# The low part of every fourth piece of weights: a subtraction on VectorE, or a DMA that adds

## The chip, the cores and the metric

The kernel runs on one core of one Trainium2 chip. The time is device microseconds of one execution. The kernel before was run three times: 2742.07, 2743.56 and 2744.54 us, a median of 2743.56.

## What is computed

The reference is a model of two times two layers on 256 tokens of width 1024, all in float32. Each of the first two layers is a gated feed-forward of hidden width 2816, a mixer of three kinds of attention (a difference of two softmaxes, a stick-breaking one, and one by blocks), and another feed-forward; the last two have a scan with decays and a dilated-window attention as their mixer. Norms stand ahead of each phase:

```
x = x + 0.5 * rms_norm(swiglu(rms_norm(x, g1), wg, wu, wd), g2)
x = x + rms_norm(mixer(rms_norm(x, g3), w_in, ...) , g4)
x = x + 0.5 * rms_norm(swiglu(rms_norm(x, g5), wg, wu, wd), g6)
```

What matters here is that every product with weights is a float32 product, and that each weight is used once, for all 256 tokens.

## The kernel before, in words

The host lays the weights out in the order of their use, as 448 units of 512 rows by 512 columns, 1 MB each. A unit makes two *pieces* of 256 rows, so there are 896 pieces; a piece is two chunks of 128 rows.

The kernel feeds TensorE with a shorter format than float32 (float32r). Each operand is split into a high part, rounded to float32r, and a low part, what the rounding left; three products (high by high, high by low, low by high) replace one. For activations this is done once for a phase. For weights it is done piece by piece, just ahead of their use:

- `fetch` (line 395) issues the DMA of a unit on SyncE's queue (SP) into one of three `raw` buffers.
- `prepare` (line 406) takes the next piece, gets a buffer each of `whi` and `wlo` (eight of each) and calls `split`. Its instructions get a lower priority than what the program puts down after them (`LATER = 200`). While a chain of norms between two phases is under way, a piece is split in two halves of 512 elements a partition.
- `split` (line 431) is two instructions: a cast on ScalarE (ACT), raw to `whi`, and a subtraction on VectorE (DVE), raw minus `whi` to `wlo`.
- `get` hands out chunks, `pump` prepares another piece when buffers are free, and is called after each step of products.

All products go through `mm` (tokens as the stationary side, 512 weight columns moving), or `across` (weights stationary, both parts of the tokens moving). In `ahead`, `branch`, `out_proj` and the end of a down projection all chunks of up to 16 are held while the first token tile passes over them, and each is released in the pass of the second.

The order of the program is made by a planner (`_Order`, line 135). The products are its main line. Other work (norms, transposes, attention heads) is in tasks, which are taken up between steps of the main line once what they read should be there, by rough lengths of the instructions that `_Eng` (line 253) reckons for each engine. A norm's last step, `rstd` (line 463), is a power on GpSimd (POOL), which does nothing else in this kernel. Behind the planner a scheduler puts each engine's instructions into queues, which run in order.

Of the kernel before, what the change touches and what calls it, by code (L numbers as in the profile page):

```python
# [28 lines left out]
def _constants():  # L29
    """tables that depend on shapes alone"""  # L30
    i = np.arange(128)
# [28 lines left out]
def _weights(m, which=None):  # L60
    """the weights in the order of their use, by 512 rows of 512 columns: [n, 128, 4, 512]"""
    out = []
# [72 lines left out]
class _Order:  # L135
    """The order of the program. A main line of products, and tasks that are taken up between its
    steps once what they read should be there, by rough lengths of the instructions (ns)."""
    MARGIN = 300.0
# [31 lines left out]
    def table(self, fn):  # L170
        """the time to change the scalar engine's function table, if this function asks for it"""
        sets = {AF.Exp: ("exp", "ln"), AF.Ln: ("ln",), AF.Silu: ("silu",), AF.Sigmoid: ("sigmoid",)}
        need = sets.get(fn[0]) if fn else None
        if need is None or self.act in need:
            return 0.0
        self.act = need[0]
        return 1300.0
# [64 lines left out]
    def flow(self, items, limit):  # L242
        """the items' tasks, so many at a time"""
        ts = []
        for g in items:
            while sum(not t.done for t in ts) >= limit:
                yield 300
            ts.append(self.spawn(g))
            yield 300
        yield from self.until(ts)  # L250


class _Eng:
    """An engine whose instructions are put down in the order's clock."""

# [3 lines left out]
    def __getattr__(self, fn):  # L259
        f, o, k = getattr(self._e, fn), self._o, self._k  # L260

        def call(*a, **kw):
# [17 lines left out]
            elif k == "A":  # L280
                cost = 190.0 + 0.84 * n + 95.0 * max(len(aps) - 2, 0) + o.table(a[2:3])
            elif k == "G":
                cost = 500.0 + 2.2 * n
            elif fn == "tensor_tensor_scan":
                cost = 80.0 + 2.1 * n
            elif fn == "reciprocal":
                cost = 100.0 + 6.3 * n
            elif fn in ("tensor_copy", "tensor_scalar", "memset") and not psum:
                cost = 70.0 + 0.55 * n
            else:  # L290
                cost = 80.0 + 1.05 * n + (80.0 if psum else 0.0)
# [5 lines left out]
class _Net:  # L297
# [4 lines left out]
    def __init__(self, tc, ctx, ap, out):  # L302
# [9 lines left out]
        self.fetched, self.units = 0, ap["weights"].shape[0]  # L312
        self.raws, self.parts, self.held = [], [], 0
        self.chains = []
        self.setup()

# [1 line left out]
    def tile(self, name, shape, dt=F32):  # L318
# [38 lines left out]

# [1 line left out]
    def setup(self):  # L359
# [33 lines left out]

# [1 line left out]
    def fetch(self):  # L395
        """the next 512 rows' transfer; the first ones in halves, to have them sooner"""
        if self.fetched < self.units and len(self.raws) <= 2 * (self.BUFS["raw"] - 1):
# [8 lines left out]
    def prepare(self):  # L406
        """the next 256 rows' parts"""
        self.fetch()
        raw = self.raws.pop(0)
        hi, lo = self.tile("whi", [2, 512], R32), self.tile("wlo", [2, 512], R32)  # L410
        n = 2 if all(t.done for t in self.chains) else 1
        with self.tc.high_priority(offset=-self.LATER):
            for i in range(0, 2, n):
                self.split(hi[:, i:i + n], lo[:, i:i + n], raw[:, i:i + n])
        self.fetch()
# [7 lines left out]
    def get(self, n=1):  # L423
        """the (hi, lo) parts of the next n times 128 rows"""
        while len(self.parts) < n:
# [8 lines left out]

# [1 line left out]
    def mm(self, out, a, b, start, stop, last):  # L436
        """in three passes over parts; last: the weights' last use"""
        (ah, al), (bh, bl) = a, b
# [9 lines left out]
    def mf(self, out, a, b, start, stop):  # L448
        """float32 as it is: products too narrow to gain from parts"""
        self.o.tensor.matmul(out, a, b, start=start, stop=stop, skip_group_check=True)  # L450
# [7 lines left out]
    def turned(self, src, n, hi, lo):  # L458
        """src [128, n*128] transposed by blocks, in two parts"""
        self.split(hi, lo, self.transposes(src, n))  # L460

# [1 line left out]
    def rstd(self, ss, n, mult, add):  # L463
        """(ss*mult + add) ** -0.5"""
        nc = self.o
# [6 lines left out]
    def rstd2(self, ss, mult, add):  # L472
        """the same of the sum of ss's two columns"""
        ms = self.t1(1, "ms2")
# [3 lines left out]
    def pre_norm(self, t, gain):  # L478
        """x's norm, in two halves, into hT as they come"""
        nc = self.o  # L480
# [19 lines left out]
    class Finish:  # L500
        """what follows a phase: its result into x, and the next phase's norm"""

# [47 lines left out]

# [1 line left out]
    def silu(self, g):  # L552
# [10 lines left out]
    def both(self, done=None):  # L563
        """the next 512 columns for both token tiles, chunk by chunk"""
        A = [self.acc() for _ in range(2)]
# [8 lines left out]
    def across(self, done):  # L574
        """the next 512 columns as channels by tokens, 128 at a time: the weights' high part
        meets both parts of the tokens at once, their products side by side in a bank"""
        A = [self.acc() for _ in range(4)]
# [20 lines left out]
    def ahead(self, prev, done):  # L598
        """the next twice 512 columns, one token tile after the other"""
        w = {}  # L600
# [85 lines left out]

# [1 line left out]
    def gates(self):  # L688
# [7 lines left out]
    def branch(self, acts, nk, sg, first, last):  # L696
        """merged (+)= sigmoid(gate) * (acts @ w); the last one's result goes on to mT"""
        nc = self.o
# [36 lines left out]

# [1 line left out]
    def values(self):  # L737
# [4 lines left out]
    def scores(self, q, k, rows, p, mask):  # L742
        """masked scores of a map per range of rows, each in a bank of its own: blocks (queries,
        keys) = (0, 0), (1, 0), (1, 1)"""
        Z = [self.tp([3, 128]) for _ in rows]
# [12 lines left out]
    def exps(self, Z, nm, sm):  # L758
        """nm: minus the maxima per query tile, sm: the sums; -> the exponentials [128, 3, 128]"""
        nc = self.o  # L760
# [13 lines left out]
    def weigh(self, O, W, V, c):  # L774
        """O [128, 2 query tiles, n] = the weights' products with columns c of the values"""
        self.mf(O[:, 0], W[:, 0], V[:, 0, c], True, True)
# [3 lines left out]
    def weigh_fm(self, Ws, V, p, T):  # L780
        """the same for a pair of heads, channels by tokens, in two parts"""
        O = self.tp([256])
# [13 lines left out]
    def head_norm(self, O, mult, add, gain, into):  # L796
        """O [128, h, 128] in PSUM: rms norm of each head times gain"""
        nc = self.o
# [8 lines left out]

# [1 line left out]
    def rope16(self, v, t):  # L809
        """v: [128, 8, 64], the first 16 of each 64 turned"""  # L810
        nc = self.o
# [9 lines left out]
    class Heads64:  # L821
        """-> [128 (pair of heads), 4 pairs, 256 tokens], turned by their positions"""

# [52 lines left out]
    def stick(self, q, k, V, T):  # L876
        """weights sigmoid(z) times the product of sigmoid(-z) over the later keys"""
        nc = self.o
# [96 lines left out]

# [1 line left out]
    def lower_bounds(self):  # L977
        """lb of layer 1 per channel, [128, 8 heads], and 1 - lb"""
        nc = self.o
# [16 lines left out]
    def hgrn_heads(self, l, b):  # L996
        """heads 4b .. 4b+3, channels by tokens: q, f, 1 - f"""
        nc = self.o
# [18 lines left out]
    def hgrn(self, qfk, vals, b, gain, o):  # L1017
        """The scan as masked products: for a key s and a query t, the decay between them is cut
        at the largest block border between the two, so that both factors are products of f
        inside a block. o: [128 tokens, 512] per token tile, before the gate."""  # L1020
        nc = self.o
# [59 lines left out]
    class Heads128:  # L1081
        """-> [128, 4 heads, 256 tokens], normed, turned by their positions"""

# [25 lines left out]
    def dilated(self, g, q, k, V, res):  # L1109
        """group g's softmax, as unscaled sums, their weights' sums and minus their maxima"""  # L1110
        nc = self.o
# [17 lines left out]
    def joined(self, res, T):  # L1129
        """the three groups' softmaxes weighted by their sums"""  # L1130
        nc = self.o
# [80 lines left out]

# [1 line left out]
    def phases(self):  # L1214
        """[(gain of the norm ahead, body(prev, finish), gain behind, half)]"""
        ap = self.ap
# [61 lines left out]
```

## Time and profile before

| | us |
|---|---|
| median of three runs | 2743.56 |
| profiled execution: span from the first to the last instruction | 2741.8 |
| the same execution's busy time: TensorE products | 2711.4 |
| VectorE | 1839.4 |
| ScalarE | 1483.1 |
| GpSimd | 93.8 |

The profiled execution's span stands for its own time: the launch around it is not in the trace, and the median of the runs is 1.8 us above the span. Engines are PE (TensorE's products), PEld (its weight loads, beside PE), DVE, ACT, POOL and SP. A tile's name stands for all of its buffers. All instructions of the other engines have one line in the profile, L293, where `_Eng` puts them down, and all products L275; so groups are told apart by tiles (`wlo`, `whi`, `raw`, `acc`, `tp`). "<-" with a time behind it is idle time of the engine, and what ended it. 487 MB came over the DMA queues, nearly all on SP's.

### The profile page before, as it was taken

To read this page: it belongs to the slowest core of one execution; us is meant where nothing else is said; L and a number is where in the kernel's file an instruction comes from. 1 tells how busy PE (TensorE), PEld (TensorE's weight loads), DVE (VectorE), ACT (ScalarE), POOL (GpSimd) and SP (SyncE) were. 2 spreads that over 40 slices of the span, in tenths; PEclk is the share of its full clock that TensorE was granted. 3 is DMA by queue.
4 is the path that set the end of the run, shared out by engine and by line. 5 is a ranking of instruction groups with operands and counts; after the bars stand their busy time and mean duration, and the time that the engine had idled before them with its cause. 6 is when DMAs were issued, how large, how long until landed. Compare 5 with 4: busy or idle time off the path is not lost.

```text
span 2741.8 us, 36153 instructions
## 1 busy us (share of the span) xinstructions
PE 2711.4 (99%) x14152; PEld 2280.3 (83%) x14152; DVE 1839.4 (67%) x2720; ACT 1483.1 (54%) x2325; POOL 93.8 (3%) x88
## 2 busy tenths in 40 slices
PE   8999999999999999999999999999999999999999
PEld 7888778888887778888887888888888888888887
DVE  6657766666657766765666778666656578786663
ACT  6545655655646554554554555555546464564562
POOL 0000000000000100000001010000000011000000
PEclk9999999999999999999999999999999999999999
DMA  7544444555555444554554344445555453335453
GB/s 273 203 173 179 153 160 183 202 197 197 188 184 186 142 160 159 220 195 170 214 191 165 142 154 149 174 169 207 187 192 196 162 199 123 127 143 200 184 192 115
DMA packets 72602, 487.31 MB, mean 178 GB/s; under 512 B 9456, under 2 KB 11376, under 8 KB 15344
## 3 DMA queue, kind: packets, MB, share of 16 engines
q1 hardware_dynamic: 72432, 485.01, 48.3%
q8 instruction: 111, 1.82, 0.3%
q14 instruction: 59, 0.48, 0.0%
HBM read 483.93 MB, written 1.05 MB: 177 GB/s over the span
## 4 chain that ended last, share of the span: by engine, by line
PE 92%; DVE 5%; issue 1%; POOL 1%; ACT 1%; DMA 1%; SPq 0%; POOLq 0%; DVEq 0%; ACTq 0%
PE acc L275 84%; PE tp L275 7%; DVE wlo L293 1%; DVE s L293 1%; POOL rstd L293 1%; DVE big L293 1%; DVE x L293 0%; DVE ssh L293 0%; DMA raw<-in_weights_dram 0%; DVE ms L293 0%; DVE half L293 0%; DMA gain<-in_attn_q_norm_dram 0%; ACT s L293 0%; ACT p L293 0%; ACT whi L293 0%
## 5 line engine op out<-in xcount | busy, mean ns | idle before, releaser
L293 DVE TENSOR_TENSOR wlo<-raw,whi 128x1024 fp32r<-128x1024 f32 (+1 forms) x941 | 1085.0, 1170 | 486.0 <-ACT whi L293 482.2
L293 ACT CAST whi<-raw 128x1024 fp32r<-128x1024 f32 (+1 forms) x941 | 933.0, 1009 | 569.9 <-PE acc L275 473.3
L275 PE MATMUL acc<-hT,whi 128*128 128x512 f32 x2688 | 941.2, 394 | 0.0
L275 PE MATMUL acc<-whi,hT 128*128 128x512 f32 x2432 | 800.4, 398 | 0.8 <-ACT hT L293 0.6
L275 PE MATMUL acc<-hT,wlo 128*128 128x256 f32 x2688 | 753.1, 280 | 0.0
L275 PE MATMUL acc<-whi,big 128*128 128x512 f32 x2048 | 646.1, 392 | 0.0
L275 PEld LDWEIGHTS acc<-hT,whi 128*128 128x128 f32 x2688 | 503.3, 187 | 111.8
L275 PEld LDWEIGHTS acc<-whi,hT 128*128 128x128 f32 x2432 | 456.9, 188 | 96.3 <-issue 1.7
L275 PEld LDWEIGHTS acc<-hT,wlo 128*128 128x128 f32 x2688 | 508.2, 189 | 0.6
L275 PE MATMUL acc<-wlo,hT 128*128 128x512 f32 x1216 | 476.1, 392 | 0.0
L275 PEld LDWEIGHTS acc<-whi,big 128*128 128x128 f32 x2048 | 384.5, 188 | 79.2 <-issue 0.3
L275 PE MATMUL acc<-wlo,big 128*128 128x512 f32 x1024 | 399.0, 390 | 0.0
L275 PEld LDWEIGHTS acc<-wlo,hT 128*128 128x128 f32 x1216 | 229.4, 189 | 42.0
L275 PEld LDWEIGHTS acc<-wlo,big 128*128 128x128 f32 x1024 | 192.4, 188 | 38.5
L293 POOL TENSOR_TENSOR rstd<-ms,nhalf 128x1 f32<-128x1 f32 (+1 forms) x84 | 93.6, 1114 | 2466.1 <-DVE ms L293 2460.8
L293 DVE TENSOR_TENSOR s<-acc,s 128x256 f32<-128x256 f32 (+1 forms) x304 | 132.0, 435 | 66.9 <-ACT s L293 60.6
L293 ACT COPY s<-acc 128x256 f32<-128x256 f32 x288 | 106.5, 370 | 122.3 <-PE acc L275 120.6
L275 PE MATMUL tp<-big 128*128 128x64 f32 (+7 forms) x896 | 114.1, 290 | 2.5 <-ACT p L293 1.3
L275 PEld LDWEIGHTS tp<-big 128*128 128x128 f32 (+4 forms) x896 | 95.1, 184 | 18.4 <-issue 5.9
L293 ACT ACTIVATE s<-acc 128x512 f32<-128x512 f32 x88 | 52.5, 597 | 105.6 <-PE acc L275 105.3
L275 PE MATMUL tp<-c_ident,s 128*128 128x128 f32 x448 | 68.9, 278 | 23.3 <-DVE s L293 18.2
L275 PEld LDWEIGHTS tp<-c_ident,s 128*128 128x128 f32 x448 | 53.0, 142 | 42.7 <-DVE s L293 21.5
(118 smaller groups left out, 1384.9 us busy)
## 6 DMA issues: line engine op xcount, KB each, us to landing
raw<-in_weights_dram SPq DMA_DIRECT2D x446, 1024.0 KB, 4.8
gain<-in_g_ffn_pre_dram SPq DMA_DIRECT2D x4, 512.0 KB, 5.2
raw<-in_weights_dram SPq DMA_DIRECT2D x4, 512.0 KB, 9.0
gain<-in_g_ffn_post_dram SPq DMA_DIRECT2D x4, 512.0 KB, 5.6
gain<-in_ffn_norm_dram SPq DMA_DIRECT2D x4, 512.0 KB, 4.2
gain<-in_g_mix_pre_dram SPq DMA_DIRECT2D x2, 512.0 KB, 6.0
gain<-in_g_mix_post_dram SPq DMA_DIRECT2D x2, 512.0 KB, 4.3
gain<-in_mix_norm_dram SPq DMA_DIRECT2D x2, 512.0 KB, 4.4
```

What stands on the lines that cost most here:

```text
L275: return f(*a, **kw)
L293: return f(*a, **kw)
```

## The change

From the ninth piece on, each piece whose number leaves 3 by division by four (counted from 0: 11, 15, ... 895; 222 pieces) gets its low part in another way. ACT casts raw to `whi` as before, in one instruction of 1024 elements a partition; ACT then writes minus `whi` into `wlo`; then a DMA issued by GpSimd reads the same 256 rows of weights from HBM and adds them to what lies in `wlo`. The unit's transfer into `raw` is unchanged. The planner reckons 1500 ns of GpSimd for the issue, and has the low part ready 5000 ns behind it. (The diff also drops comments and docstrings.)

```diff
+            elif k == "G" and fn == "dma_start":
+                o.op("G", 1500.0, out, ins)
+                o.ready[_name(out)] = o.last[_name(out)] = o.free["G"] + 5000.0
+                return f(*a, **kw)
             elif k == "G":
                 cost = 500.0 + 2.2 * n
...
-        self.raws, self.parts, self.held = [], [], 0
+        self.raws, self.parts, self.held, self.prepared = [], [], 0, 0
...
         n = 2 if all(t.done for t in self.chains) else 1
+        u, self.prepared = self.prepared, self.prepared + 1
         with self.tc.high_priority(offset=-self.LATER):
-            for i in range(0, 2, n):
-                self.split(hi[:, i:i + n], lo[:, i:i + n], raw[:, i:i + n])
+            if u >= 8 and u % 4 == 3:
+                self.split_by_dma(hi, lo, raw, self.ap["weights"][u // 2][:, u % 2 * 2:u % 2 * 2 + 2])
+            else:
+                for i in range(0, 2, n):
+                    self.split(hi[:, i:i + n], lo[:, i:i + n], raw[:, i:i + n])
...
+    def split_by_dma(self, hi, lo, raw, src):
+
+        self.o.scalar.copy(hi, raw)
+        self.o.scalar.activation(lo, hi.bitcast(F32), AF.Copy, scale=-1.0)
+        self.o.gpsimd.dma_start(lo, src, accum_op=OP.add)
```

## Rows read from the trace of the kernel before

**Rows 1.** The page's engines: busy us, share of the span, instructions.
```profile
PE 2711.4 (99%) x14152; PEld 2280.3 (83%) x14152; DVE 1839.4 (67%) x2720; ACT 1483.1 (54%) x2325; POOL 93.8 (3%) x88
```
**Rows 2.** Busy time by stretch; PEclk is the granted clock, DMA the engines' busy share.
```profile
core 0: us, PE busy (x) PEld busy (x) DVE busy (x) ACT busy (x) POOL busy (x), PEclk, DMA share, GB/s
20.00:2730.00 2710.00, 2694.35 (x14084) 2267.11 (x14083) 1828.79 (x2701) 1472.14 (x2308) 92.49 (x82) 1.00 0.49 177
```
**Rows 3.** PE's waits between 20 and 2730 us: us, times, longest.
```profile
PE tp L275 <- DVE s L293: 7.8, 9, 1.2
PE tp L275 <- DVE ms L293: 3.8, 4, 1.7
PE tp L275 <- ACT p L293: 1.3, 2, 0.7
PE tp L275 <- DVE big L293: 1.1, 4, 0.4
PE tp L275 <- DVE half L293: 1.0, 1, 1.0
```
**Rows 4.** ACT's casts of weights in the waits of all engines.
```profile
ACT whi L293 <- PE acc L275: 473.3, 450, 5.3
...
ACT whi L293 <- DMA raw<-in_weights_dram: 25.9, 19, 5.3
```
**Rows 5.** Timeline (start, us taken): casts and first reads, pieces 167 and 603.
```profile
503.83 2.00 ACT L293 CAST whi<-raw 128x1024 fp32r<-128x1024 f32 x2 [2.45 <-PE acc L275]
...
521.96 0.28 PE L275 MATMUL acc<-hT,wlo 128*128 128x256 f32 x1
...
1842.30 1.06 ACT L293 CAST whi<-raw 128x1024 fp32r<-128x1024 f32 x1 [0.31 <-PE acc L275]
...
1851.15 0.28 PE L275 MATMUL acc<-hT,wlo 128*128 128x256 f32 x1
```
**Rows 6.** Groups by form: count, busy us, mean ns, idle before.
```profile
L293 DVE TENSOR_TENSOR wlo<-raw,whi 128x1024 fp32r<-128x1024 f32 x851 | 1027.8, 1221 | 486.0 <-ACT whi L293 482.2
...
L293 ACT CAST whi<-raw 128x1024 fp32r<-128x1024 f32 x851 | 882.7, 1051 | 564.5 <-PE acc L275 469.3 <-issue 65.8 <-DMA raw<-in_weights_dram 25.9
...
L293 ACT CAST whi<-raw 128x512 fp32r<-128x512 f32 x90 | 50.5, 615 | 5.4 <-PE acc L275 4.0 <-ACT s L293 1.4
```
**Rows 7.** Timeline of a joint between two phases, by engine.
```profile
643.87 0.68 DVE L293 TENSOR_TENSOR wlo<-raw,whi 128x512 fp32r<-128x512 f32 x1
644.47 0.14 DVE L293 TENSOR_SCALAR ms<-ms 128x1 f32<-128x1 f32 x1
...
643.15 3.73 ACT L293 CAST whi<-raw 128x512 fp32r<-128x512 f32 x7
...
646.46 0.66 PE L275 MATMUL tp<-c_ident,s 128*128 128x128 f32 x4 [1.08 <-DVE s L293]
```
**Rows 8.** POOL's powers, the tile `rstd`: ns min/median/max, first and last start.
```profile
L293 POOL TENSOR_TENSOR rstd<-ms,nhalf x84: 548/1006/2449, 8.9 to 2558.7; 128x1 f32<-128x1 f32 x52, 128x4 f32<-128x4 f32 x32
```
**Rows 9.** Timeline of one of these powers, and of VectorE beside it.
```profile
652.25 1.40 POOL L293 TENSOR_TENSOR rstd<-ms,nhalf 128x1 f32<-128x1 f32 x1 [6.63 <-DVE ms L293]
...
652.02 1.22 DVE L293 TENSOR_TENSOR wlo<-raw,whi 128x1024 fp32r<-128x1024 f32 x1
```
**Rows 10.** DMA queues (packets, MB, share); issues (count, KB, us to landing).
```profile
q1 hardware_dynamic: 72432, 485.01, 48.3%
...
raw<-in_weights_dram SPq DMA_DIRECT2D x446, 1024.0 KB, 4.8
...
out_dram<-x SPq DMA_DIRECT2D x4, 256.0 KB, 2.0
```
**Rows 11.** The tile `raw`: SP's issues in ns, then the transfers' time to landing.
```profile
L293 SPq DMA_DIRECT2D raw<-in_weights_dram x450: 327/328/1037, 2.6 to 2702.5; - x150
...
DMA to landing us min/median/max: 4.6/4.8/11.7
```
**Rows 12.** Busy time in a stretch behind a pass that held sixteen chunks.
```profile
466.00:471.00 5.00, 5.00 (x24) 4.14 (x23) 4.56 (x6) 1.50 (x5) 1.40 (x1) 1.00 0.85 316
```

## The prediction

> **What bounds the kernel now.** I read the shares of the engines first: VectorE (DVE) is busy for 67% of the span and ScalarE (ACT) for 54% [rows 1]. Then the same by stretch: between 20 and 2730 us TensorE (PE) is busy for 2694.35 of 2710.00 us [rows 2]. So 15.7 us are idle there; the other 15 us of idle time are the start and the end, which the change, beginning at the ninth piece, leaves alone. The list of PE's waits in that stretch says what the 15 us are: five entries, 15.0 us, every one in front of a product that writes a `tp` bank (transposes and attention), none for the parts of weights [rows 3]. VectorE's subtraction, however long, is not waited for. TensorE's granted clock in it was 1.00, the 2.4 GHz level [rows 2].
>
> **How far ahead the weights are.** A piece (256 rows) is cast by ACT into one of eight `whi` buffers as soon as PE has read the piece that had the buffer before: 450 casts waited for PE, 473.3 us in all [rows 4]. The time from a cast's end to PE's first read of the same piece's `wlo` is the room that a slower way to make the low part has. I paired casts and products by counting them along their engines. Of the 896 pieces the change touches 222 (numbers 11, 15, ... 895). Piece 167, a usual one, is the second cast of its row, ends at 505.83 and is first read at 521.96: 16.1 us, which is the median. Piece 603, the tightest, ends at 1843.36 and is read at 1851.15: 7.8 us [rows 5]. Of the 222, 4 have under 8 us, 15 under 9, 36 under 10, 44 under 12, 58 under 14, 92 under 16, 170 under 18. The tight ones stand behind passes that hold sixteen 128-row chunks for the first token tile and release them, fast, during the second.
>
> **The change part by part.** All sums are against the profiled execution, 2741.8 us of span; the median of the runs is 1.8 us more, and I add these 1.8 at the end.
>
> *Removed:* 222 subtractions of 1.22 us [rows 6], some 271 us of VectorE. In the bulk nobody waits for them: worth nothing. At the joints between phases, where a norm runs through ACT, VectorE and GpSimd (POOL) while PE runs out of work, a little comes back. There PE stood still 1.08 us for the normed `s`, and just before it a `ms` of the same norm had stood behind a 0.68 us subtraction [rows 7]. The power on POOL stood too: issued 0.23 us into a 1.22 us subtraction it took 1.40 us, where the shortest of its kind takes 0.55 [rows 8, 9]. There are 11 joints. A quarter of (1.22 + 0.85) us at each is 5.7 us, the most that can come back; 0 is the least; I take 2, because most of what a norm waits for is itself.
>
> The Trainium skill, "SBUF — State Buffer", section "Who interferes with whom", says that a DVE instruction with two SBUF inputs contends with a GpSimd instruction that reads SBUF but not with one that only writes it; the POOL row agrees for the reading half (1.40 against 0.55 us). By that rule the writing of a DMA's descriptors on POOL isn't held by a subtraction; if it is held like the power it costs up to 0.99 us more a DMA, which is priced below as part of the lag.
>
> *Added on ACT:* 222 copies with a factor of -1 of 128x1024. Nearest row: the cast of that shape, 1.05 us [rows 6], together 233 us, ACT 54 to 63%. In the bulk ACT waits for PE anyway [rows 4]. At a joint it can cost: seven half casts stand in a row there, 3.73 us, beside the norm's own work [rows 7]. Normally the piece is cast in two halves of 0.62 us during a chain of norms [rows 6]; a piece of the new kind takes two whole instructions of 1.05: 2.1 instead of 1.2 us, 0.9 more on ACT before a norm's next step. Eleven joints with 0 to 0.9 us each, 0 to 10 us; I take 4, a little under half, since not each piece stands ahead of a step that PE waits for.
>
> *Added on POOL and its queue:* 222 issues. The trace has none. Below: SP's issue of a weight transfer, 0.33 us; above: POOL's longest power, 2.45 us. I take 1.0, POOL's median [rows 8, 11]. Behind such an issue only POOL's 84 powers can be queued; who waits for them is the norm's next product on VectorE, and PE behind that (a rival below).
>
> *Added to the DMA engines:* 222 times 0.52 MB from HBM, added to what lies in `wlo`. Before: 485.01 MB took 48.3% of the engines [rows 10], so 116 MB more is 12%, or 23% if the destination has to be read as well. 71% in all: the engines don't become the bound on that count. Time from issue to landing: below, the 256 KB store, 2.0 us; above, the longest weight transfer, 11.7; nearest, a 1 MB transfer, 4.8, since 0.5 MB of source and 0.5 MB of destination are 1 MB of reading [rows 10, 11]. But the tight places are those where the raw buffers are being refilled: the share of the DMA engines was 0.85 in such a stretch [rows 12]. So I take 6.0.
>
> The Trainium skill, "DMA: Bandwidth & Descriptors", section "Anatomy of one DMA — SWDGE (gpsimd) path", gives 2.0 us plus the bytes over 436 GB/s, by its figures an estimate of 4.4 us for 1 MB read; no run here shows it for an adding transfer, and by it no piece would be late.
>
> *The added wait:* PE's product with `wlo` now waits for copy + issue + landing behind the cast: 1.05 + 1.0 + 6.0 = 8.05 us; ends 1.05 + 0.33 + 2.0 = 3.4 and 1.05 + 2.45 + 11.7 = 15.2. I walked through the 222 leads in order, each stall of PE pushing later casts and reads alike. PE's stalls then sum to: lag up to 7.8 us, nothing; 8 us, 0.7 us (4 pieces); 9 us, 10.6 (15); 10 us, 28 (35); 11 us, 57 (42); 12 us, 90 (43); 15.2 us, 216 (53). What is queued behind a stalled product is all of PE. I take the 8.05 and 1 us.
>
> *Moved:* the raw half is free after the cast, not after the subtraction, so SP may issue some fetches 1.2 us earlier; PE doesn't wait for raw (ACT does, 25.9 us, hidden by the leads [rows 4]): nothing. The planner that writes the order counts 1500 + 5000 ns for the new DMA: in its clock some pieces come late, and it may place a transpose of a norm a step sooner or later. I put this into the bounds of the ACT term at the joints (-4 to +10 more) with a middle of 0.
>
> Sum: 2741.8 - 2 + 4 + 1 = 2744.8, with the 1.8 us 2746.6, say **2747**: 0.1% above, within what can be told from no change (0.2%, 5.5 us).
>
> **The rivals.**
>
> 1. *The low part lands too late* (slower). One mechanism: a lag above 7.8 us stalls PE at the tight places behind the passes that hold sixteen chunks. It decides from about 8.6 us on, where it costs over 5 us. For it: landing took up to 11.7 us, and in these places the engines are filled with raw transfers. Against: the usual 1 MB landing is 4.8 us. With a lag of 10 to 11.5 us: 2747 + 27 to 73, 2774 to 2820.
>
> 2. *POOL as a queue* (slower). A power behind an issue that waits for ACT's copy comes later by up to copy plus issue, 2.1 us, at 11 joints: +23, 2770. For it: POOL runs in order, and at the joint ACT's casts and the norm's powers fall into the same 5 us [rows 7]. Against: most of the 222 issues fall between joints, with no power near.
>
> 3. *The joints get shorter* (faster). VectorE freed from the subtraction lets the powers through: POOL's rows show it held by one [rows 9]. With all 5.7 us, no ACT cost and no late piece: 2738; with the planner's 4 as well, 2734. Against: the quarter that goes is seldom the one in the way, and ACT pays more than VectorE gets.
>
> 4. *The adding is slow in the DMA engines themselves.* At five times the engine time of a byte, 58% beside the 48.3%, the engines are over full: 2742 x 1.06 = 2910 and more. Nothing in the trace bears on an adding transfer; only the factor of two has a reason in it.
>
> **How the numbers follow.** Forecast as summed 0.47, rival 1 0.30, rival 2 0.10, rival 3 0.10, rival 4 0.03. Faster by over 0.2% is rival 3: 0.10; within 0.2% the forecast: 0.47; slower by over 0.2% the rest: 0.43. The likeliest case alone reaches from 2740 to 2750 (its terms at -4 to +5 us). The range goes down to 2738, the forecast's terms with the joints' whole gain, and up to 2790, a lag of 10.5 us; beyond it lie the later part of rival 1 (0.06), rival 4 and the lower end of rival 3 (0.03).
>
> **What would show it.** VectorE's `wlo` group should fall by 222 instructions and some 271 us, ACT grow by some 233 us, POOL's queue show 222 issues with their time to landing. Step by step: if issue to landing is near 6 us and PE's list of waits still has no entry for weights, the forecast's path is right. An entry of PE for a DMA or for `wlo`, in stretches like 1843 to 1856 us, is rival 1; its size against the landing time tests the table of lags. Longer waits of PE in front of the `tp` transposes, with POOL's or ACT's new instructions ahead of the norm, are rival 2 or a larger ACT term; shorter ones are rival 3. A DMA share near 1 would be rival 4. The forecast is wrong if the time leaves 2738 to 2749 for any of these, and wrong in its reason if it stays while PE waits for `wlo`.

## The result and the profile after

The changed kernel took 2808.9 us (median of four runs, 2805.7 to 2812.1) against 2743.9 (four runs): 1.0238 times as long, 95% interval 1.0226 to 1.0249, or 65 us more. The forecast was 2747, and at most 2790. The first rival, a low part that lands too late, is what happened, within its price of 2774 to 2820 us.

What the change says it does it does: VectorE's subtractions of whole pieces fell from 851 to 642 and those of halves from 90 to 64, which is 222 pieces fewer:

```profile
L297 DVE TENSOR_TENSOR wlo<-raw,whi 128x1024 fp32r<-128x1024 f32 x642 | 778.5, 1222 | 594.1 <-ACT whi L297 593.6
L297 DVE TENSOR_TENSOR wlo<-raw,whi 128x512 fp32r<-128x512 f32 x64 | 41.3, 683 | 0.0
```

VectorE's whole busy time fell by 243 us, ACT's grew by 209, POOL's by 179 (page: busy time of the engines, then the DMA queues with packets, MB and share of the engines; q0 is POOL's; to compare with [rows 1, 10]):

```profile
PE 2733.9 (97%) x14152; PEld 2289.3 (81%) x14152; DVE 1596.4 (57%) x2485; ACT 1691.7 (60%) x2530; POOL 272.6 (10%) x310
...
q1 hardware_dynamic: 72432, 485.01, 48.6%
q0 software_dynamic: 31968, 116.41, 22.6%
```

PE is busy for 22.5 us more though it has the same 14152 products, and the span is 68.2 us longer, so it stands idle for 45.7 us more. Its waits between 20 and 2800 us, where those of before had no entry for weights [rows 3]:

```profile
PE acc L275 <- DMA wlo<-in_weights_dram: 42.0, 17, 6.5
PE tp L275 <- DVE s L297: 8.6, 12, 1.3
PE acc L275 <- DVE s L297: 4.3, 3, 2.1
PE tp L275 <- ACT p L297: 4.0, 5, 1.4
PE tp L275 <- DVE big L297: 0.6, 2, 0.4
PE tp L275 <- DVE ms L297: 0.4, 2, 0.2
```

The first line is new, and alone nearly the whole of the added idle time (42.0 of 44.4 us in the program); the rest adds up to 18 us, where it was 15. The third line is new too, and not for weights: ahead of the two longest of its three waits VectorE stood for small tables from HBM, which it never did for these tables in the kernel before:

```profile
DVE lbm L297 <- DMA logits<-in_hgrn_lb_logits_dram: 4.4, 1, 4.4
DVE c_dil L297 <- DMA s<-in_c_dil_dram: 4.0, 2, 2.1
```

In what follows the *lead* of a piece is the time from its cast's end to PE's first read of its `wlo` in the trace of before, and the *lag* the time from its cast's end until the low part has landed. The terms of the lag, read from the tile `wlo` (ns min/median/max of ACT's copy and of POOL's issue; then issue to landing in us):

```profile
L297 ACT ACTIVATE wlo<-whi x222: 1042/1060/1104, 36.4 to 2785.3; 128x1024 fp32r<-128x1024 f32 x111
L285 POOL DMA_DIRECT2D wlo<-in_weights_dram x222: 862/865/1022, 37.8 to 2786.7; - x111
...
DMA to landing us min/median/max: 5.3/7.1/11.5
```

The landing is counted from the start of POOL's issue, which it contains. Copy and issue are as reckoned. The landing is not, and its median doesn't tell the worst: over the 19 pieces for which PE waited until they landed (its products for 17, its weight loads alone for two more), the landing took 6.6 to 11.5 us (median 9.7), and the lag behind the cast was 8.0 to 14.3 us (median 11.1).

One such place, piece 71 (timeline of PE, then POOL, then SP):

```profile
216.05 0.61 PE L275 MATMUL acc<-whi,hT 128*128 128x512 f32 x2
222.99 0.79 PE L275 MATMUL acc<-wlo,hT 128*128 128x512 f32 x1 [6.33 <-DMA wlo<-in_weights_dram]
...
211.61 0.89 POOL L285 DMA_DIRECT2D wlo<-in_weights_dram  x1 [7.38 <-ACT wlo L297]
...
209.35 4.54 SPq L297 DMA_DIRECT2D raw<-in_weights_dram  x3
213.95 0.79 SPq L297 DMA_DIRECT2D gain<-in_g_mix_post_dram  x1
```

The adding DMA, issued at 211.61, lands at 222.94. Around it SP issues three 1 MB raw transfers and a 512 KB row of gains; PE stops for 6.3 us. The stretches around this stop (columns as in [rows 2]):

```profile
216.00:223.00 7.00, 0.67 (x4) 0.21 (x3) 1.78 (x4) 0.17 (x2) 0.55 (x1) 0.83 1.00 318
223.00:229.00 6.00, 6.00 (x21) 4.84 (x22) 0.98 (x2) 1.49 (x3) 0.00 (x0) 0.63 0.33 115
```

The DMA engines are busy for all of the first stretch. When PE goes on, it does so at a granted clock of 0.63 in the mean: the 1.2 GHz level for a part of it, where the matmul at 222.99 takes 0.79 us instead of 0.39. Over the run the record of the clock has seven such stretches ahead of the kernel's end, 3.4 to 6.8 us long, 38 in all, each begun during or just behind a wait of PE of 2.1 us or more (six times for `wlo`, once behind VectorE's wait for a table); PE worked for 27 of the 38, which is 13 us lost. The forecast had no such term.

Piece 71 is one of four (71, 151, 283 and 363), all at joints between phases, that make 24.6 of the 42.0 us of waits and, with 8.5 us of the clock behind them, half of the loss. In these four the landing took 10.3 to 11.5 us, and other work of ACT stands for 1.43 us between the cast and the copy, where at the median of the 222 pieces it is 0.03 us.

So the 68 us of span are 44 us of PE's idle time in the program, 13 by the clock, 1.3 at the start and the end, and some 9 that I can't place.

What the third rival hoped for can be seen on POOL, whose narrow powers fell from 0.86 to 0.64 us in the mean (before, then after), but not in PE's time:

```profile
L293 POOL TENSOR_TENSOR rstd<-ms,nhalf 128x1 f32<-128x1 f32 x52 | 44.6, 857 | 2006.4 <-DVE ms L293 2003.8 <-DVE s L293 2.6
L297 POOL TENSOR_TENSOR rstd<-ms,nhalf 128x1 f32<-128x1 f32 x52 | 33.0, 636 | 275.2 <-DVE ms L297 275.1
```

### The profile page after: what moved, and what is told of

Same layout as the page of the kernel before. It is cut to its first block, busy times and chain, and to the rows that moved or that the text cites. A ratio compares the mean times of both kernels' runs of the same rounds, so it can differ in the third digit from the quotient of the medians.

```text
span 2810.0 us, 36412 instructions
## 1 busy us (share of the span) xinstructions
PE 2733.9 (97%) x14152; PEld 2289.3 (81%) x14152; DVE 1596.4 (57%) x2485; ACT 1691.7 (60%) x2530; POOL 272.6 (10%) x310
## 3 DMA queue, kind: packets, MB, share of 16 engines
q1 hardware_dynamic: 72432, 485.01, 48.6%
q0 software_dynamic: 31968, 116.41, 22.6%
## 5 line engine op out<-in xcount | busy, mean ns | idle before, releaser
L297 DVE TENSOR_TENSOR wlo<-raw,whi 128x1024 fp32r<-128x1024 f32 (+1 forms) x706 | 819.3, 1174 | 594.1 <-ACT whi L297 593.6
L285 POOL DMA_DIRECT2D wlo<-in_weights_dram x222 | 193.7, 872 | 2076.3 <-ACT wlo L297 1420.2
L297 ACT ACTIVATE wlo<-whi 128x1024 fp32r<-128x1024 f32 x222 | 235.4, 1061 | 5.9
L297 POOL TENSOR_TENSOR rstd<-ms,nhalf 128x1 f32<-128x1 f32 (+1 forms) x84 | 79.0, 941 | 438.4 <-DVE ms L297 421.7
```

Of the source, the lines that this page charges most:

```text
L285: return f(*a, **kw)
L297: return f(*a, **kw)
```

## The experiments

All were timed in three rounds beside the kernel before. Lines that the diffs leave out are the changed kernel's. The waits in the last column are those of one execution, the profiled one; for the plain copy that was its fastest (2764.9 of 2764.9 to 2779.8 us).

| run | us | ratio to before, 95% | PE's waits for `wlo`, us |
|---|---|---|---|
| changed kernel | 2808.9 | 1.0226 to 1.0249 | 42.0 |
| ACT's copies alone | 2747.6 | 1.0006 to 1.0025 | none |
| planner as before | 2809.7 | 1.0225 to 1.0257 | 43.9 |
| not where tight | 2750.3 | 1.0016 to 1.0036 | none |
| only where tight | 2808.2 | 1.0225 to 1.0256 | 43.7 |
| first halves | 2801.9 | 1.0181 to 1.0243 | 40.2 |
| plain copy | 2772.2 | 1.0082 to 1.0126 | 17.7 |
| half the raws | 2777.6 | 1.0110 to 1.0143 | 20.2 |
| plain copy, half the raws | 2755.2 | 1.0026 to 1.0054 | 8.3 |
| one chunk | 2778.5 | 1.0111 to 1.0141 | 22.0 |

**ACT's copies alone.**

```diff
-        self.o.gpsimd.dma_start(lo, src, accum_op=OP.add)
+        self.o.vector.tensor_tensor(lo, raw, hi.bitcast(F32), op=OP.subtract)
```

> ACT still writes minus the high part into wlo for the 222 pieces, but VectorE then subtracts as before and overwrites it; no DMA is issued by GpSimd. Left in of the change: only ACT's 222 extra copies. Theory 1 (the low part lands late, because of the DMA): back to 2744 to 2750 us, PE's list of waits without an entry for weights, granted clock 1.00. Rival (ACT's extra 233 us hold up the norms and the casts): 2780 us or more, without any DMA.

It took 2747.6 us, 4.3 more than before. PE's waits (20 to 2730 us) have no line for weights:

```profile
PE tp L275 <- DVE s L297: 11.2, 16, 1.3
PE tp L275 <- ACT p L297: 1.7, 3, 0.7
```

ACT's busy time was 1687.9 us, 205 more than before. The copies cost 4 us (1.6 to 6.9 by the interval), with the old subtractions still behind them, and the other 61 come with the DMA.

**The planner's part.** The DMA is put down without the planner's knowledge:

```diff
...
+            self.o.op("A", 190.0 + 0.84 * 512 * n, h, [r])
+            self.o.op("V", 80.0 + 1.05 * 512 * n, l, [r, h])
+        nc.scalar.copy(hi, raw)
+        nc.scalar.activation(lo, hi.bitcast(F32), AF.Copy, scale=-1.0)
+        nc.gpsimd.dma_start(lo, src, accum_op=OP.add)
```

> The same instructions as the changed kernel, but the planner reckons each of the 222 pieces as a cast and a subtraction, so the order of the products and tasks is that of the kernel before. Theory 1: no change to speak of, 2795 to 2815 us, PE waits for wlo of 40 us or more. Rival (the planner, which has the low part ready 5000 ns behind the issue, spoils the order of the work around the joints): 2750 to 2770 us.

2809.7 us, as the changed kernel. The planner's idea of the DMA has no part in the loss that these runs could show.

**Where the loss is.** The 222 in two parts, by the lead that each piece had before; `TIGHT` is the list of the 45 numbers:

```diff
-            if u >= 8 and u % 4 == 3:
+            if u >= 8 and u % 4 == 3 and u not in TIGHT:
```
```diff
-            if u >= 8 and u % 4 == 3:
+            if u in TIGHT:
```

> The 45 pieces whose lead in the trace of before was under 12.2 us (all but one or two of them behind passes that hold sixteen chunks) are subtracted on VectorE again; the other 177 keep the adding DMA. Theory 1 (only the tight places lose): 2744 to 2756 us, no wait of PE for wlo over 1 us, clock 1.00. Rival (the loss is spread over all pieces, through the DMA engines' 23% or ACT's copies): four fifths of the loss stay, some 2790 to 2800 us.

> The opposite: only those 45 pieces have the adding DMA, one fifth of the changed kernel's DMAs. Theory 1: nearly the whole loss stays, 2785 to 2810 us, with PE's waits for wlo of 30 us or more and the clock at its lower level behind the long ones. Rival (spread): one fifth of the loss, 2750 to 2760 us.

2750.3 and 2808.2 us. With 177 adding DMAs, whose queue still took 18.7% of the engines, the kernel is 6.7 us slower than before, which can't be told from the 4.3 us of ACT's copies (the intervals overlap). With the other 45 it is as slow as with all. PE's waits of the two, in this order:

```profile
PE tp L276 <- DVE s L298: 8.5, 11, 1.2
PE tp L276 <- ACT p L298: 4.2, 6, 1.2
PE tp L276 <- DVE ms L298: 3.8, 4, 1.7
PE acc L276 <- DVE s L298: 2.5, 3, 1.0
PE tp L276 <- DVE big L298: 0.9, 3, 0.4
```
```profile
PE acc L276 <- DMA wlo<-in_weights_dram: 43.7, 14, 6.6
PE tp L276 <- DVE s L298: 10.6, 11, 1.5
```

The landings of the 177 (5.4/7.4/12.4 us) are no shorter than those of the 45 (5.4/7.5/11.6): what tells them apart is the lead. This is the clearest result here: the loss is a matter of the lead at a few places, not of how much the adding DMAs move in all.

**Why it lands late there.** First the unit's own next transfer:

```diff
-            if u >= 8 and u % 4 == 3:
+            if u >= 8 and u % 4 == 2:
```

> Pieces whose number leaves 2, not 3, by division by four: the first half of a unit, whose cast doesn't free the raw buffer, so that SP doesn't issue the next 1 MB just ahead of the adding DMA. The number of pieces (222), the work and the leads of the tight places stay. Theory 1b (it is the raw transfer issued just before that the adding DMA shares the engines with): landing falls to 5.5 to 6.5 us at the median and the time to 2760 to 2785 us. Theory 1a (the adding alone): 2800 to 2815 us, landing about 7.

2801.9 us, with PE's waits at 40.2. The landing's median fell to 6.6, its longest grew to 12.5, and at the tight places it was 8.6 to 12.5. For the pieces just ahead of the 19 the landing's median was 8.7 us, where it was 9.7 for the 19, and the time can't be told from the changed kernel's. The leads are nearly, not quite, as tight as those of the 222 (28 under 10 us instead of 36). So the transfer that the same piece's cast sets free is a small part at most. Then the adding itself, and the raw transfers as such:

```diff
-        self.o.gpsimd.dma_start(lo, src, accum_op=OP.add)
+        self.o.gpsimd.dma_start(lo, src)
```

> The DMA copies the weights into wlo and adds nothing, so the low part holds the weights themselves, a changed computation; issue, queue, waits and bytes from HBM are those of the changed kernel. The changed kernel's adding queue took 22.6% of the engines for 116.41 MB, 1.94 times what a byte cost on SP's queue. Theory 1a (half of the engine time is the adding's, and it is this that makes the landing late): queue share about 11.6%, landing 4.5 to 5.5 us at the median, PE waits for wlo under 10 us, 2746 to 2760 us. Theory 1b (the raw transfers in the same queue engines make it late, whatever the DMA does): landing still 8 to 10 us at the tight places, 2780 to 2805 us.

```diff
-            raw = self.tile("raw", [4, 512])
-            src = self.ap["weights"][self.fetched]
...
+            if self.fetched < 2 or self.fetched % 2 == 0:
+                raw = self.raw = self.tile("raw", [4, 512])
+                src = self.ap["weights"][self.fetched]
...
+            raw = self.raw
```

> Every second unit after the first two isn't transferred: its two pieces are cast from the raw buffer of the unit ahead of it, so half of the raw traffic is left out and the products use wrong weights. All else is the changed kernel's, the 222 adding DMAs too. Theory 1b (at the tight places the adding DMA is late because raw refills share the DMA engines): its landing there falls from 9 to 11.5 us to 5.5 to 7 us, PE's waits for wlo under 10 us, 2750 to 2765 us. Theory 1a (the adding by itself is that slow): landing as before, 2795 us or more.

> Both at once: the DMA copies and doesn't add, and every second unit isn't transferred (half of the raw traffic left out, and the products use wrong weights). If the adding's second read and the raw refills together make the lag at the tight places, the lag falls to 6.5 to 8 us there, PE's waits for wlo to under 4 us, the clock stays at 1.00 and the time is 2747 to 2757 us: ACT's copies (4 us) and a little. If something else of the DMA path (its issue on GpSimd, its wait, its semaphores) has a share of its own, some of the 29 us that the plain copy still cost stay: 2762 us or more.

Neither theory alone had it. The plain copy leaves 29 us of the 65, half the raws 34, both together 12. The queues and landings of the plain copy, of half the raws, then of both together:

```profile
q1 hardware_dynamic: 72432, 485.01, 47.9%
q0 software_dynamic: 31968, 116.41, 12.8%
...
DMA to landing us min/median/max: 3.7/5.6/11.2
```
```profile
q0 software_dynamic: 31968, 116.41, 23.1%
...
DMA to landing us min/median/max: 5.3/6.9/10.9
```
```profile
q0 software_dynamic: 31968, 116.41, 12.5%
...
DMA to landing us min/median/max: 3.7/5.4/7.7
```

Without the adding the queue needs 12.8% of the engines instead of 22.6%, and the shortest landing is 3.7 us instead of 5.3. Leaving out half of the raw transfers takes the longest landing from 11.2 to 7.7 us where the DMA only copies, but only from 11.5 to 10.9 where it adds. Over the same 19 pieces the landing's median was 9.7 us in the changed kernel, 7.7 with the plain copy, 8.1 with half the raws and 5.8 with both: 2.1 and 1.6 us shorter by themselves, 3.9 together. So the lag at the tight places has both causes, and they add up there; 0.33 of the 2.1 us are POOL's shorter issue, 0.53 us for 0.86.

With both gone the profiled execution is 12 us longer than that of before. Of these 8.3 us are waits, and the clock fell three times behind them, for 3.4 us each, which costs 5 more; that is all of it, and ACT's 4 us aren't seen beside them. The waits are at the four joints, where 1.43 us pass between ACT's cast and its copy because other work of ACT stands in between, so that the lag is 9.4 to 10.4 us with a landing of 6.6 to 7.7. The time is in the range that I expected, but the waits (under 4 us) and the lag there (6.5 to 8) are not.

**Half the size.**

```diff
-        self.o.scalar.activation(lo, hi.bitcast(F32), AF.Copy, scale=-1.0)
-        self.o.gpsimd.dma_start(lo, src, accum_op=OP.add)
+        self.o.scalar.activation(lo[:, :1], hi[:, :1].bitcast(F32), AF.Copy, scale=-1.0)
+        self.o.gpsimd.dma_start(lo[:, :1], src[:, :1], accum_op=OP.add)
+        self.o.vector.tensor_tensor(lo[:, 1:], raw[:, 1:], hi[:, 1:].bitcast(F32), op=OP.subtract)
```

> In the 222 pieces only the first of the two chunks is made by ACT's copy (512 elements a partition) and the adding DMA (256 KB); VectorE subtracts the second. Theory 1 (the lag against the lead decides): copy 0.6 instead of 1.06 us and landing some 2 us earlier, a lag shorter by 2.5 to 3 us; by the table of lags 2752 to 2770 us. Rival (a fixed cost for each adding DMA, whatever its size, is what hurts): 2790 to 2810 us.

2778.5 us, outside what I had expected of either side. The shortest landing fell to 3.9 us, the median to 6.5, and the median over the same 19 pieces from 9.7 to 7.4: some 2 us, as expected, and the time stayed under the rival's 2790. But PE still waited for landings of up to 9.5 us, and at the four joints ACT's other work between cast and copy is 1.3 to 2.9 us, so that the lag over the 19 fell by 1.7 us and not by 2.5 to 3.

None of these versions is faster than the kernel before, and the first view says why: its idle time between 20 and 2730 us is 16 us, and none of it is put down to the subtraction.

## Why the prediction was wrong, point by point

- *PE is the bound, and VectorE's 271 us are worth nothing in the bulk*: right. The relief at the joints (2 us) can't be told apart in any run: PE's waits for `ms` fell from 3.8 to 0.4 us, but those for the normed `s` rose from 7.8 to 8.6 and those for `p` from 1.3 to 4.0.
- *ACT's copies, 4 us*: right as far as it can be told, 4.3 (1.6 to 6.9) measured with the subtractions left in.
- *POOL's issue, 1.0 us*: 0.87. But it stood in the sum twice, since the landing as the profile counts it contains the issue; behind the copy the issue began after 0.29 us. The Trainium skill, "SBUF — State Buffer", section "Who interferes with whom", has a VectorE instruction with two SBUF inputs contend with a GpSimd instruction that reads SBUF, not with one that only writes it, and the prediction took the issue for one that writes. The trace agrees: ten issues began during a subtraction and took 0.92 us at most; the other 212 had a median of 0.86. Rival 2, POOL as a queue, is not seen either: only two of the 84 powers follow right behind an issue, each 0.16 us after its `ms`, and no wait of PE grew by the rival's price.
- *The planner*: 0 was right, as far as its run shows.
- *Landing, "I take 6.0"*: the step that failed. It was a term of the sum; the mechanism beside it was right: the wait, the threshold of 7.8 us, and the places (of the 19 pieces that PE stood for, 18 have a lead of under 10 us in the trace of before, one of 12.1). At those places it took 9.7 us at the median. I had taken one 1 MB transfer and a quarter more for the company; there two to four raw transfers are under way before the low part lands (at piece 71 three, and a row of gains), and all of them, with the adding's double cost, pass in the same ten microseconds. My own row had a share of 0.85 and a longest landing of 11.7 [rows 11, 12]; I chose by the median of a transfer that mostly runs alone.
- *The copy right behind the cast*: a term put at nothing. That was so at most places, but at the four joints with the longest waits it measured 1.43 us, which came on top of the longest landings.
- *The first rival's price* came out by luck. By the table of lags 11.1 us, the median measured at the 19 pieces, gives some 60 us, close to the measured 65; but these 60 were meant as PE's waits alone, at 42 pieces. Measured were 42 us at 19 pieces, and 13 came from the clock, for which I had no term.
- The Trainium skill, "DMA: Bandwidth & Descriptors", section "Anatomy of one DMA — SWDGE (gpsimd) path", gave an estimate of 4.4 us for 1 MB read. The shortest adding landing was 5.3 us and the median 7.1, so that by its formula the lag comes out shorter, and further off, than by the rows of the trace; 19 pieces were late, where by it none would be.
- The range ended at 2790, a lag of 10.5 us, while the bounds of the landing reached to 11.7 us and those of the lag to 15.2: the upper bound was written down and then not kept.

## What to carry to other kernels

Where work moves to a path of long latency, look for the places with the shortest lead and take the latency that holds *there*, with the transfers that are in flight at that moment: places that release many buffers at once are both where the leads are short and where the queues are full. A fifth of the moved pieces made the whole loss here, and taking work off an engine that nobody waited for gained nothing. Count also what stands between the steps of the new path: at the four worst places it was other work of ACT. When TensorE is made to wait, count the clock behind the wait as well as the wait.

## What the runs showed of the hardware that was not expected

- The adding DMAs took 22.6% of the engines for 116.41 MB, SP's queue, nearly all raw transfers, 48.6% for 485.01: 1.94 times as much for a byte. The same queue without adding took 12.8% of a shorter span, so in engine time the adding DMA costs 1.80 times the copy. The Trainium skill, "Collectives: The Full Stack", section "The bandwidth ceiling: the fold count and why AG ≠ RS ≠ AR", puts ReduceScatter's half speed against AllGather down to the add's two source reads; a ratio near two agrees with that, but no run here tells the second read from the add itself.
- POOL's issue took 0.86 us with adding and 0.53 without (plain copy: 527/528/693 ns, min/median/max).
- In the changed kernel TensorE fell to the 1.2 GHz level for 6.8 us during waits of 5.6 to 6.5 us, and during or behind waits of 2.1 to 2.9 us for 3.4 us or not at all (one of 2.5 us had none). With the planner as before a wait of 3.2 us had none either. In the kernel before, with no wait over 1.7 us after the start, it had 1.00 until 2740 us.
